# Binary cross-entropy over 8192 x 8192: the last big store moves to GpSimd's queue, and two of the three closing clips move behind other work on VectorE

## The chip, the core and the metric

One core of a Trainium2 chip runs the whole program. The metric is the device time of one execution in microseconds, median of the runs shown; lower is better. The kernel uses VectorE (DVE) and ScalarE (ACT) for arithmetic. Transfers between the device memory and the on-chip memory are issued by GpSimd (POOL), SyncE (SP) and, at the very start, ScalarE, and are carried out by the core's 16 DMA engines.

## What is computed

Two matrices of 8192 x 8192 float32, `pred` in (0.01, 0.99) and `target` of zeros and ones:

```
pred = clip(pred, 1e-7, 1 - 1e-7)
out  = -(target * log(pred) + (1 - target) * log(1 - pred))
```

Because `target` is 0 or 1, the kernel computes it as `-log(|target - 1 + pred|)`: for a target of 1 the argument is `pred`, for a target of 0 it is `|pred - 1|`.

## The kernel before

The matrices are treated as one flat run of elements and cut into 36 chunks, numbered k = 0 to 35. A chunk takes the same number of columns on each of 128 partitions: two chunks of 3072 columns, 31 of 16384 (k = 2 to 32, the big ones, 8 MiB of `pred` each), two of 4608 and one of 1024. The last three (k = 33, 34, 35) are called a, b and c in the code and "the small chunks" here.

Two rings in on-chip memory hold the data: `ring_p` in float32 (it takes `pred`, is worked on in place, and is stored as the result) and `ring_t` in bfloat16 (`target`, converted by its load). Each ring has two slots of 16384 columns and a spare of 1024. The big chunks use the two slots in turn. Chunk 31 lies in slot 0, chunk 32 in slot 1. The small chunks a and b lie side by side in slot 0, where chunk 31 was, and c lies in the spare, which nobody used before.

A chunk goes through five operations, each in place:

- `clip` (L89, VectorE), the two bounds in one instruction
- `log`, three instructions: `target - 1 + pred` (L95, VectorE), absolute value (L98, ScalarE), natural logarithm (L99, ScalarE)
- `back` (L103, VectorE), the change of sign

The big chunks are worked on in eight pieces of 2048 columns: clip and log of each piece in turn, and then back of all eight, and then one store. Chunks a and b are clipped whole and otherwise worked on in halves of 2304 columns; c is worked on whole.

The order on every engine is the order of the program text; nothing reorders it. What is loaded ahead is issued by GpSimd, one queue for all of it: in the loop's step k it issues the `target` and then the `pred` load of chunk k + 1, and then, when VectorE has finished with chunk k, its store (`store`, L80). In the last step (k = 32) it issues instead the three `target` loads of a, b, c (L76), and then their three `pred` loads (L73). The `pred` load of a waits until the store of chunk 31, whose slot it takes, has landed. GpSimd's queue, `q0` in the profile, takes up the issued transfers in the order of issue. The function `store` picks the queue: the last four stores (k = 32 to 35) are SyncE's, `q1` in the profile, and all others are GpSimd's. SyncE also waits in order: a store that it issues stands behind the one before it.

The end of the program (L134 to L148) is the part that the change touches: first the three clips of a, b and c, one after the other, and then the logs and backs of the small chunks, with the stores of a, b and c. The store of c is cut by rows into three issues (L85).

Of the kernel before, what the change touches and what calls it, by code (L numbers as in the profile page):

```python
# [1 line left out]

# [4 lines left out]

EPS = 1e-7

BIG = 16 * 1024  # L10
FIRST = 3072
LAST = 4608
TAIL = 1024
SLOTS = 2
PIECES = 8


def plan(total):
    n = (total - 2 * FIRST - 2 * LAST - TAIL) // BIG
    assert n > 4 and total == 2 * FIRST + n * BIG + 2 * LAST + TAIL  # L20
    spots = [(FIRST, 0, 0), (FIRST, FIRST, FIRST)]
    spots += [(BIG, k % SLOTS * BIG, k % SLOTS * BIG) for k in range(1, n + 1)]
    end = (n + 1) % SLOTS * BIG
    spots += [(LAST, end, end), (LAST, end + LAST, end + LAST)]
    return spots + [(TAIL, SLOTS * BIG, SLOTS * BIG)]


@with_exitstack
def kernel(
    ctx: ExitStack,  # L30
    tc: tile.TileContext,
    pred: bass.AP,
    target: bass.AP,
    out: bass.AP,
):
    nc = tc.nc
    fp32 = mybir.dt.float32
    bf16 = mybir.dt.bfloat16
    Alu = mybir.AluOpType
    Act = mybir.ActivationFunctionType  # L40
    P = nc.NUM_PARTITIONS

    R, C = pred.shape
    spots = plan(R * C // P)
    n = len(spots)
    widths = [s[0] for s in spots]
    cols = [sum(widths[:k]) for k in range(n)]

    def chunk(ap, k):
        flat = ap.rearrange("r c -> (r c)")  # L50
        return flat[cols[k] * P : (cols[k] + widths[k]) * P].rearrange("(p w) -> p w", p=P)

    pool = ctx.enter_context(tc.tile_pool(name="rings", bufs=1))
    ring_p = pool.tile([P, SLOTS * BIG + TAIL], fp32, name="ring_p", tag="ring_p")
    ring_t = pool.tile([P, SLOTS * BIG + TAIL], bf16, name="ring_t", tag="ring_t")
    warm = pool.tile([1, 8], fp32, name="warm", tag="warm")

    def spot(k, part=(0, 1)):
        w, c, _ = spots[k]
        i, m = part  # L60
        return ring_p[:, c + i * w // m : c + (i + 1) * w // m]

    def spot_t(k, part=(0, 1)):
        w, _, c = spots[k]
        i, m = part
        return ring_t[:, c + i * w // m : c + (i + 1) * w // m]

    def load_p(k):
        if k == 0:
            for rows in (slice(0, P, 2), slice(1, P, 2)):  # L70
                nc.scalar.dma_start(out=spot(0)[rows], in_=chunk(pred, 0)[rows])
        else:
            nc.gpsimd.dma_start(out=spot(k), in_=chunk(pred, k))  # L73

    def load_t(k):
        nc.gpsimd.dma_start(out=spot_t(k), in_=chunk(target, k))  # L76

    def store(k):
        queue = nc.sync if k >= n - 4 else nc.gpsimd
        queue.dma_start(out=chunk(out, k), in_=spot(k))  # L80

    def store_rows(k):
        src, dst = spot(k), chunk(out, k)
        for first, last in ((0, 108), (108, 120), (120, 128)):
            nc.sync.dma_start(out=dst[first:last], in_=src[first:last])  # L85

    def clip(k, *part):
        p = spot(k, *part)
        nc.vector.tensor_scalar(  # L89
            out=p, in0=p, scalar1=EPS, scalar2=1 - EPS, op0=Alu.max, op1=Alu.min  # L90
        )

    def log(k, *part):
        p = spot(k, *part)
        nc.vector.scalar_tensor_tensor(  # L95
            out=p, in0=spot_t(k, *part), scalar=1.0, in1=p, op0=Alu.subtract, op1=Alu.add
        )
        nc.scalar.activation(out=p, in_=p, func=Act.Abs)  # L98
        nc.scalar.activation(out=p, in_=p, func=Act.Ln)  # L99

    def back(k, *part):
        p = spot(k, *part)
        nc.vector.tensor_scalar(out=p, in0=p, scalar1=-1.0, scalar2=None, op0=Alu.mult)  # L103

    with tc.manual_schedule():
        nc.vector.memset(warm, 1.0)  # L106
        load_t(0)
        load_p(0)
        load_t(1)
        for k in (1, 2):  # L110
            load_p(k)
        load_t(2)
        nc.scalar.activation(out=warm, in_=warm, func=Act.Ln)  # L113
        for k in (0, 1):
            clip(k)
            log(k)
        for k in (0, 1):
            back(k)
            store(k)
        a, b, c = range(n - 3, n)  # L120
        m = PIECES
        for k in range(2, a):
            coming = (k + 1,) if k + 1 < a else (a, b, c)
            for j in coming:
                load_t(j)
            for j in coming:
                load_p(j)
            for i in range(m):
                clip(k, (i, m))
                log(k, (i, m))  # L130
            for i in range(m):
                back(k, (i, m))
            store(k)
        for j in (a, b, c):  # L134
            clip(j)
        log(a, (0, 2))
        log(a, (1, 2))
        log(b, (0, 2))
        back(a, (0, 2))
        log(b, (1, 2))  # L140
        back(a, (1, 2))
        store(a)
        log(c)
        back(b, (0, 2))
        back(b, (1, 2))
        store(b)
        back(c)
        store_rows(c)  # L148


# [1 line left out]
_INS = ['pred', 'target']  # L152
_OUTS = [((8192, 8192), 'float32')]


# [23 lines left out]
```

## Time and profile before

| what | value |
|---|---|
| time, median of 3 runs | 1886.07 us (1885.7 to 1886.33) |
| the profiled execution's own time | 1886.53 us |
| its span, from the first to the last instruction | 1884.7 us |
| VectorE busy | 1171.3 us (62%) |
| ScalarE busy | 954.8 us (51%) |
| HBM read and written over the span | 536.87 MB and 268.44 MB, 427 GB/s |
| transfers of GpSimd's queue q0, SyncE's q1, ScalarE's q10 | 655.89, 13.63 and 1.57 MB |

How to read it: times inside the execution are counted from the start of the span. An instruction's busy time is the time in which its engine worked on it; a transfer is not an instruction, and shows as the time from its issue to its landing. The share of the 16 DMA engines that is busy is given by stretches; values a little over 1 occur, because a stretch counts packets that overlap. The transferred bytes of a `target` load are counted at bfloat16's size, half of what is read from memory, so the GB/s of a stretch with such loads looks low while the DMA engines are fully busy.

The order of instructions around the end, by the trace: chunk 32's last back ends at 1827.16 us; SyncE issues its store at 1827.19 us. The three small `pred` loads are issued between 1809.87 us and 1812.42 us.

### The profile page before, as it was taken

What the parts mean: (1) busy time and instruction counts of PE and PEld (TensorE: products, weight loads), DVE (VectorE), ACT (ScalarE), POOL (GpSimd) and SP (SyncE); (2) the same over time, 40 slices, a digit from 0 to 9 for tenths busy, and PEclk for the clock granted to TensorE, in tenths of its full rate; (3) what the DMA queues carried; (4) which work ended last, traced back from release to release, by engine and by line L of the source; (5) the groups of instructions that cost most, each with busy time, mean ns of one, the idle gap of its engine ahead of it and who ended that gap; (6) DMA issues with size and microseconds to landing.
All of it is one profiled execution on the core that took longest, in us unless ns stands there. A gap on an engine that the chain in (4) does not pass through costs nothing.

```text
span 1884.7 us, 1546 instructions
## 1 busy us (share of the span) xinstructions
DVE 1171.3 (62%) x764; ACT 954.8 (51%) x512; POOL 56.4 (3%) x107
## 2 busy tenths in 40 slices
DVE  3775556755567655577555775556765567755584
ACT  2664336653456544566444664446654456634463
POOL 0000000000000000000000000000000000000000
DMA  9999999999999999999999999999999999999994
GB/s 333 301 334 401 378 349 341 352 371 399 345 353 337 365 392 370 341 351 341 398 378 352 340 351 376 396 353 345 344 362 394 369 344 346 347 392 385 346 369 205
DMA packets 15595, 671.19 MB, mean 356 GB/s; under 512 B 1760, under 2 KB 1760, under 8 KB 2400
## 3 DMA queue, kind: packets, MB, share of 16 engines
q0 software_dynamic: 14832, 655.89, 97.1%
q1 hardware_dynamic: 592, 13.63, 1.7%
q10 hardware_dynamic: 160, 1.57, 0.2%
q14 instruction: 11, 0.09, 0.0%
HBM read 536.87 MB, written 268.44 MB: 427 GB/s over the span
## 4 chain that ended last, share of the span: by engine, by line
DMA 38%; issue 30%; DVE 30%; ACT 1%; POOL 1%; POOLq 0%; DVEq 0%; PEldq 0%
DMA ring_p<-in_pred_dram 34%; DVE ring_p L95 15%; DVE ring_p L89 7%; DVE ring_p L103 7%; DMA out_dram<-ring_p 4%; ACT ring_p L99 1%; ACT ring_p L98 0%; POOL ring_t L76 0%; POOL out_dram L80 0%; POOL ring_p L73 0%; POOLq L80 0%; DVEq L95 0%; PEldq L174 0%; POOLq L73 0%; POOLq L76 0%
## 5 line engine op out<-in xcount | busy, mean ns | idle before, releaser
L98 ACT ACTIVATE ring_p<-ring_p 128x2048 f32<-128x2048 f32 (+2 forms) x255 | 485.1, 1902 | 910.4 <-DVE ring_p L95 910.4
L89 DVE TENSOR_SCALAR ring_p<-ring_p 128x2048 f32<-128x2048 f32 (+2 forms) x253 | 312.1, 1233 | 667.6 <-DMA ring_p<-in_pred_dram 667.6
L95 DVE SCALAR_TENSOR_TENSOR ring_p<-ring_t,ring_p 128x2048 f32<-128x2048 bf16 (+2 forms) x255 | 586.4, 2300 | 27.3 <-DMA ring_t<-in_target_dram 18.8
L99 ACT ACTIVATE ring_p<-ring_p 128x2048 f32<-128x2048 f32 (+2 forms) x255 | 489.0, 1918 | 8.1
L103 DVE TENSOR_SCALAR ring_p<-ring_p 128x2048 f32<-128x2048 f32 (+2 forms) x255 | 293.8, 1224 | 9.0 <-ACT ring_p L99 9.0
L73 POOL DMA_DIRECT2D ring_p<-in_pred_dram x35 | 19.6, 562 | 1209.4 <-DMA out_dram<-ring_p 1209.4
L80 POOL DMA_DIRECT2D out_dram<-ring_p x32 | 17.2, 537 | 545.6 <-DVE ring_p L103 545.6
L76 POOL DMA_DIRECT2D ring_t<-in_target_dram x36 | 19.8, 551 | 0.8 <-PEq L174 0.8
L113 ACT ACT_TABLE_LOAD x1 | 1.3, 1283 | 2.0 <-issue 2.0
L106 DVE MEMSET warm<- 1x8 f32 x1 | 0.1, 65 | 0.8 <-PEq L163 0.8
L113 ACT ACTIVATE warm<-warm 1x8 f32<-1x8 f32 x1 | 0.2, 208 | 0.0
L163 POOL MEMSET const-float32-0.0<- 128x1 f32 x1 | 0.1, 98 | 0.2 <-issue 0.2
L163 POOL MEMSET const-bfloat16-1.0<- 128x1 bf16 x1 | 0.1, 101 | 0.0
L163 POOL MEMSET const-float32-1.0<- 128x1 f32 x1 | 0.1, 99 | 0.0
L163 POOL MEMSET const-uint8-127<- 128x1 uint8 x1 | 0.1, 98 | 0.0
## 6 DMA issues: line engine op xcount, KB each, us to landing
ring_t<-in_target_dram POOLq DMA_DIRECT2D x31, 4096.0 KB, 58.9
ring_p<-in_pred_dram POOLq DMA_DIRECT2D x2, 2304.0 KB, 23.5
out_dram<-ring_p SPq DMA_DIRECT2D x2, 2304.0 KB, 7.2
out_dram<-ring_p POOLq DMA_DIRECT2D x2, 1536.0 KB, 35.0
ring_t<-in_target_dram POOLq DMA_DIRECT2D x2, 1152.0 KB, 47.5
ring_p<-in_pred_dram ACTq DMA_DIRECT2D x2, 768.0 KB, 6.9
ring_t<-in_target_dram POOLq DMA_DIRECT2D x2, 768.0 KB, 11.5
ring_p<-in_pred_dram POOLq DMA_DIRECT2D x1, 1536.0 KB, 16.1
```

Source lines behind the costliest of these rows:

```text
L73: nc.gpsimd.dma_start(out=spot(k), in_=chunk(pred, k))
L76: nc.gpsimd.dma_start(out=spot_t(k), in_=chunk(target, k))
L80: queue.dma_start(out=chunk(out, k), in_=spot(k))
L89: nc.vector.tensor_scalar(out=p, in0=p, scalar1=EPS, scalar2=1 - EPS, op0=Alu.max, op1=Alu.min)
L95: nc.vector.scalar_tensor_tensor(out=p, in0=spot_t(k, *part), scalar=1.0, in1=p, op0=Alu.subtract, op1=Alu.add)
L98: nc.scalar.activation(out=p, in_=p, func=Act.Abs)
L99: nc.scalar.activation(out=p, in_=p, func=Act.Ln)
L103: nc.vector.tensor_scalar(out=p, in0=p, scalar1=-1.0, scalar2=None, op0=Alu.mult)
L106: nc.vector.memset(warm, 1.0)
L113: nc.scalar.activation(out=warm, in_=warm, func=Act.Ln)
L163: nc = _bacc.Bacc("TRN2", target_bir_lowering=False, num_devices=1)
```

## The change

Two edits.

In `store`, the bound for SyncE's queue moves by one, so that the store of chunk 32 is GpSimd's. In GpSimd's order it comes behind the three `pred` loads of a, b and c, as its last transfer. SyncE is left with the stores of a, b and c.

At the end of the program the three clips no longer stand together. The clip of a stays where it was. The clip of b moves behind both additions (L95) of a, right in front of b's first. The clip of c moves behind the first store, right in front of c's addition. Nothing else moves, and no operation is added or removed.

```diff
     def store(k):
-        queue = nc.sync if k >= n - 4 else nc.gpsimd
+        queue = nc.sync if k >= n - 3 else nc.gpsimd
         queue.dma_start(out=chunk(out, k), in_=spot(k))
...
-        for j in (a, b, c):
-            clip(j)
+        clip(a)
         log(a, (0, 2))
         log(a, (1, 2))
+        clip(b)
         log(b, (0, 2))
         back(a, (0, 2))
         log(b, (1, 2))
         back(a, (1, 2))
         store(a)
+        clip(c)
         log(c)
         back(b, (0, 2))
         back(b, (1, 2))
```

## The prediction

> **What bounds the kernel now.** I read the shares of the page first: VectorE is busy 62% and ScalarE 51% of the span, while the row of DMA slices is 9 (90% or more) in every slice but the last, which is 4. So the kernel is bound by its transfers up to the last slice of 47 us, and both edits lie there. The view of busy time by stretches, over the end (columns: stretch, its length, busy time of VectorE, ScalarE and GpSimd, granted clock, DMA share, GB/s):
>
> ```profile
> 1770.00:1790.00 20.00, 0.00 (x0) 0.00 (x0) 1.62 (x4) 1.00 1.02 442
> ...
> 1840.00:1847.00 7.00, 2.56 (x1) 0.00 (x0) 0.00 (x0) 1.00 1.02 441
> 1847.00:1849.00 2.00, 0.00 (x0) 0.00 (x0) 0.00 (x0) 1.00 0.24 100
> 1849.00:1851.00 2.00, 0.00 (x0) 0.00 (x0) 0.00 (x0) 1.00 0.08 35
> 1851.00:1853.30 2.30, 0.02 (x1) 0.00 (x0) 0.00 (x0) 1.00 0.02 7
> 1853.30:1866.40 13.10, 13.10 (x8) 9.87 (x5) 0.00 (x0) 1.00 0.00 0
> ...
> 1881.00:1882.50 1.50, 0.00 (x0) 0.00 (x0) 0.00 (x0) 1.00 0.70 227
> 1882.50:1883.50 1.00, 0.00 (x0) 0.00 (x0) 0.00 (x0) 1.00 0.49 184
> 1883.50:1884.70 1.20, 0.00 (x0) 0.00 (x0) 0.00 (x0) 1.00 0.00 0
> ```
>
> The engines that move data are full until 1847, then all but one or two are done (0.08 of 16 engines is 1.3), and one trails until about 1853. From 1853.3 to 1866.4 nothing at all is moved, while VectorE is busy throughout. Why VectorE is busy only then stands in the timeline:
>
> ```profile
> 1827.34 2.56 DVE L89 TENSOR_SCALAR ring_p<-ring_p 128x4608 f32<-128x4608 f32 x1 [0.18 <-DMA ring_p<-in_pred_dram]
> 1840.01 2.56 DVE L89 TENSOR_SCALAR ring_p<-ring_p 128x4608 f32<-128x4608 f32 x1 [10.11 <-DMA ring_p<-in_pred_dram]
> 1853.28 0.69 DVE L89 TENSOR_SCALAR ring_p<-ring_p 128x1024 f32<-128x1024 f32 x1 [10.71 <-DMA ring_p<-in_pred_dram]
> 1853.88 7.49 DVE L95 SCALAR_TENSOR_TENSOR ring_p<-ring_t,ring_p 128x2304 f32<-128x2304 bf16 x3
> 1856.47 2.12 ACT L98 ACTIVATE ring_p<-ring_p 128x2304 f32<-128x2304 f32 x1 [32.55 <-DVE ring_p L95]
> ```
>
> Chunk a is clipped at 1827.34, but its addition stands behind the clips of b and c, which wait 10.11 and 10.71 us for their loads. ScalarE idles 32.55 us with it. The loads of b and c are late because the big store runs beside them from 1827.19. That is in the list of transfers (size, median us from issue to landing):
>
> ```profile
> ring_p<-in_pred_dram POOLq DMA_DIRECT2D x2, 2304.0 KB, 23.5
> out_dram<-ring_p SPq DMA_DIRECT2D x2, 2304.0 KB, 7.2
> ring_p<-in_pred_dram POOLq DMA_DIRECT2D x1, 512.0 KB, 42.4
> ...
> out_dram<-ring_p SPq DMA_DIRECT2D x1, 25.6
> ```
>
> The last row is the big store (8192 KB): 1827.19 + 25.6 = 1852.8. The 512 KB load of c was issued at 1810.90 and landed 42.4 later, at 1853.25, with the store.
>
> **The change, part by part.** First the rate. The store of chunk 31 ran alone on the DMA engines after the load of 32 (landed 1790.28, where VectorE's next clip begins) until 1809.58 (the chain of waits): 8192 KB in 19.3 us, 424 KB/us. Between 1827.3 (a landed) and 1853.2 the loads of b and c and the big store moved 2304 + 512 + 8192 = 11008 KB in 25.9 us, 425 KB/us. These are times of the trailing engine, which ends each of them; 424 is its pace, times 16.
>
> *The store's queue.* One issue of 0.54 us (GpSimd's mean for L80) leaves SyncE and joins GpSimd. In GpSimd's queue it passes no one: the three loads are issued by 1812.42, before chunk 32 is ready at 1827.2, and behind it stands only the end of the program. In front of SyncE's store of a stands nothing now. The bytes are the same, but they are taken up in another order: b's load needs 2304 / 424 = 5.4 us after a, so it lands at 1832.7 instead of 1840.0; c's 1.2 more, 1833.9 instead of 1853.25; and then the big store, 19.3, until 1853.2, as before. Cover for a late start of it: the trailing engine has loads until 1833.9, 6.7 us after the issue; other engines end their loads some 5 us earlier (the trail in the stretches from 1847 to 1853) and would idle first, which costs nothing as long as the trailing one is not caught up.
>
> *The clips.* VectorE from 1827.34, durations of the same shapes (clip 2.56, addition 7.49 / 3 = 2.50, back 1.35; for c 0.69, 1.22, 0.69): clip a to 1829.9; additions of a to 1832.4 and 1834.9; clip b (landed 1832.7, no wait) to 1837.5; b's first addition 1840.0; back of a's first half 1841.3 (ScalarE is done with it at 1832.4 + 2 x 2.12 = 1836.7); b's second addition 1843.8; back of a's second half 1845.2, and a's store is issued, 21.2 us earlier than its 1866.4 now. Clip c to 1845.9 and its addition to 1847.1, with up to 0.5 for the gap that stood between clip c and the next addition (1853.45 to 1853.88 in the chain). ScalarE goes from 1840.9 through b's halves, done at 1845.2 and 1849.4, and c, done at 1851.5. Back of b's second half then ends at 1850.8 and b's store is issued (now 1874.7); back of c at 1852.2 (now 1876.0). Removed: the two waits, 20.8 us on the path. Added: no instruction and no wait; clip b and c cost the same 2.56 and 0.69 as before, now beside transfers instead of behind them.
>
> *What sets the end then.* Not that chain: the transfers. A store takes about 7.2 - 5.4 = 1.8 us more than its bytes, so a's data flow from about 1847, inside the big store; b's from 1852.6, before the trailing engine can be through with the big store and a (1853.2 + 5.4 = 1858.6); c's likewise. So the trailing engine never idles, and it is done at 1853.2 + 4608 / 424 (10.9) + c's part. An even share of c is 512 / 424 = 1.2; a cut into 108, 12 and 8 rows need not be even over 16 engines, so the bound below is 0. I take the middle, 0.6: 1864.7. From the last transfer to the end of the span it was about 1.1 (busy to 1883.5 or a little more, end at 1884.7). Span 1865.8, 18.9 less than 1884.7. With the 1.83 that lie around the span (1886.53 - 1884.7) the profiled execution would take 1867.6; the median of the runs lies 0.46 below the profiled one, so **1867.2**.
>
> The Trainium skill, "DMA: Bandwidth & Descriptors", section "Latency and other measured facts", states that DMA engines 7 and 15 are usually slower than the rest; and its section "Why a DMA increments its semaphore by 16 and not by 1", that a transfer issued by SyncE runs on the lowest-numbered engines, as many as divide its partitions, 12 for 108. The trailing engine of the rows above fits the first; if it is 15, c's part on it is 0 and the time 1866.6; if it is 7, 512 / 12 KB at a sixteenth of 424 are 1.6, and the time is 1868.2.
>
> Bounds of what the trace does not show, a store of GpSimd's beside one of SyncE's: full pace on one side; on the other the 409 GB/s of the stretch 1829 to 1840, where loads of the one queue met the store of the other, against 441 after it, over the 18 us from 1847: 1.4 more. If a last piece of 64 KB of the big store (65536 bytes, one row of 16384 columns) stood by itself at the end, 64 / 26.5 = 2.4 more. Below: c's part 0 and the tail 0.7, 1 less, and some spread.
>
> **Rivals.**
>
> *The queue's order does not matter* (the change does not do the first thing it says): the loads land as before, 1840.0 and 1853.25. For it: a queue's transfers overlap where pieces are small. Against: the loads of a and b came one after the other. VectorE then clips b to 1842.6 and issues a's store at 1850.3; clip c, its addition and b's backs end near 1858.4, b's data flow from 1859.8, 1.2 after the trailing engine is free: 1868.4. The clips alone bring nearly all.
>
> *The store's start is held up by VectorE.* GpSimd issues it at 1827.2, exactly when VectorE takes up clip a, and VectorE then works without a break to 1852. The three load issues at 1809.87, beside a busy VectorE, took 2.55 us against 1.61 for the three at 1770.02 beside an idle one; whether their data also came later is hidden by the backlog. If it were held until VectorE's last back, the trailing engine would idle from 1833.9 until a's store at 1846.6, 12.7 us, and the time be 1867.2 + 12.7 + 1 = 1880.9. Against it: each big load of the loop is issued amid VectorE's work (at 1751.91 between pieces), and the DMA share stays at 0.94 or more. The Trainium skill, "SBUF — State Buffer", section "SBUF: two separate sides", names this: while VectorE runs in a mode that uses the port it shares with GpSimd, GpSimd cannot write descriptors. By that rule a single clip holds it for 2.56 us, which the 6.7 us of cover take.
>
> *Two queues of stores disturb each other, slower than before.* Place: from 1846.6 on, where a's store meets the rest of the big one. Left to move then: 6.6 us of the big store and 5120 KB, 18.7 us at full pace. The old traffic ended at 1883.5, 36.9 us later; so it decides at half the pace, some 215 KB/us. At 0.45 of it the time is 1890. For it: no row shows two queues of stores at once. Against: the loads of one beside the store of the other ran at 409 and 441 GB/s.
>
> **How the numbers follow.** Forecast 0.86, loads as before 0.06 (1868.4), start held up 0.04 (up to 1880.9), stores disturbing each other 0.04 (near 1886 or above). The likeliest gives 1867.2. Up to 1871.5 for the 1.4 and 2.4 of the bounds, down to 1864.5; that takes in the first rival and leaves out less than 2 in 10. A measurement of this kernel tells 0.2%, 3.8 us, from no change. Faster by more: the first three cases, 0.96; of the last, 0.01 within 0.2% and 0.03 slower.
>
> **What would show it.** Right: clip a followed at once by two additions; clip b with no wait and c's load landed by about 1834; a's store issued near 1845 and c's near 1852; no stretch between 1827 and 1864 with a DMA share near 0; the last instruction near 1866. Wrong: clip c waiting for its load (the order of the queue), a hole in the DMA share between 1834 and 1846 (start held up), GB/s well under 400 from 1847 to 1859 with all engines busy (stores disturbing each other), or VectorE or ScalarE still at work after 1860.

## The result, and the profile after

The changed kernel takes 1869.12 us (median of 4 runs, 1868.35 to 1869.34), the kernel before beside it 1886.2 us (1885.7 to 1887.71). The ratio is 0.9907, with a 95% interval of 0.989 to 0.9925: 17.1 us less. The forecast was 1867.2 us in a range of 1864.5 to 1871.5. The profiled execution of the changed kernel took 1868.35 us, its span 1866.6 us.

The timeline of its end (start, length, engine, line, tile, shape, idle time before):

```profile
1826.27 2.56 DVE L89 TENSOR_SCALAR ring_p<-ring_p 128x4608 f32<-128x4608 f32 x1 [0.18 <-DMA ring_p<-in_pred_dram]
1826.38 2.57 POOL L80 DMA_DIRECT2D out_dram<-ring_p  x1 [15.05 <-DVE ring_p L103]
1828.86 5.03 DVE L95 SCALAR_TENSOR_TENSOR ring_p<-ring_t,ring_p 128x2304 f32<-128x2304 bf16 x2
...
1833.81 2.55 DVE L89 TENSOR_SCALAR ring_p<-ring_p 128x4608 f32<-128x4608 f32 x1
...
1843.88 0.69 DVE L89 TENSOR_SCALAR ring_p<-ring_p 128x1024 f32<-128x1024 f32 x1
...
1843.99 6.11 SPq L80 DMA_DIRECT2D out_dram<-ring_p  x2
...
1851.03 4.19 SPq L85 DMA_DIRECT2D out_dram<-ring_p  x3
```

Of the three clips only a's has an idle time in front of it, 0.18 us; the 10.11 and 10.71 us of before are gone. The first small store is issued at 1843.99 instead of 1866.4, c's at 1851.03 instead of 1876.05. The second line is GpSimd's issue of the big store; it took 2.57 us, as long as the clip beside it, where such issues took 0.54 us on average before.

The transfers (size, median us from issue to landing):

```profile
ring_p<-in_pred_dram POOLq DMA_DIRECT2D x2, 2304.0 KB, 19.9
out_dram<-ring_p SPq DMA_DIRECT2D x2, 2304.0 KB, 14.0
ring_p<-in_pred_dram POOLq DMA_DIRECT2D x1, 512.0 KB, 23.1
...
out_dram<-ring_p POOLq DMA_DIRECT2D x1, 27.2
```

The load of c, issued at 1809.8 behind those of a and b, landed 23.1 us later, at 1832.9 (1853.25 before). The big store landed at 1826.38 + 27.2 = 1853.6. Everything at the end of this execution lies some 1.1 us earlier than in the kernel before (a's clip at 1826.27 for 1827.34), so by the distance from a's clip it landed later: 27.3 us for 1852.8 - 1827.34 = 25.5. A small store now takes 14.0 us to land for 7.2: it is issued early and waits its turn.

The busy time by stretches (stretch, length, VectorE, ScalarE, GpSimd, granted clock, DMA share, GB/s). A stretch counts a DMA packet wholly where the packet begins, and a row of the big store is one packet of 2.4 us, so a share can be over 1, and too low in the stretch behind:

```profile
1829.00:1846.60 17.60, 17.53 (x10) 15.02 (x8) 0.00 (x0) 1.00 1.07 462
1846.60:1859.00 12.40, 2.55 (x3) 3.64 (x3) 0.00 (x0) 1.00 0.89 379
1859.00:1861.00 2.00, 0.00 (x0) 0.00 (x0) 0.00 (x0) 1.00 0.85 285
1861.00:1863.00 2.00, 0.00 (x0) 0.00 (x0) 0.00 (x0) 1.00 0.55 193
1863.00:1865.00 2.00, 0.00 (x0) 0.00 (x0) 0.00 (x0) 1.00 0.06 23
1865.00:1866.60 1.60, 0.00 (x0) 0.00 (x0) 0.00 (x0) 1.00 0.01 3
```

VectorE works through the first stretch beside the transfers. The 13 us with no transfer at all are gone, and the arithmetic is over at 1851, 15 us ahead of the end. What is left at the end is a DMA share of 0.06 from 1863 to 1865, about one engine of 16. The landings in the trace agree: 15 engines are through with the store of c by 1863.7, and the last one lands at 1865.7.

### The profile page after: what moved, and what is told of

The parts are those of the page before. It is cut to its first block, busy times and chain, and to the rows that moved or that the text cites. A ratio compares the mean times of both kernels' runs of the same rounds, so it can differ in the third digit from the quotient of the medians.

```text
span 1866.6 us, 1546 instructions
## 1 busy us (share of the span) xinstructions
DVE 1171.4 (63%) x764; ACT 954.8 (51%) x512; POOL 59.0 (3%) x108
## 4 chain that ended last, share of the span: by engine, by line
DMA 37%; issue 30%; DVE 30%; ACT 1%; POOL 1%; POOLq 0%; DVEq 0%; PEldq 0%
DMA ring_p<-in_pred_dram 33%; DVE ring_p L95 15%; DVE ring_p L89 8%; DVE ring_p L103 7%; DMA out_dram<-ring_p 4%; ACT ring_p L99 1%; ACT ring_p L98 0%; POOL ring_t L76 0%; POOL out_dram L80 0%; POOLq L80 0%; DVEq L89 0%; PEldq L175 0%; POOLq L73 0%; POOLq L76 0%
## 5 line engine op out<-in xcount | busy, mean ns | idle before, releaser
L95 DVE SCALAR_TENSOR_TENSOR ring_p<-ring_t,ring_p 128x2048 f32<-128x2048 bf16 (+2 forms) x255 | 586.6, 2301 | 27.3 <-DMA ring_t<-in_target_dram 18.7
```

The costliest lines, as they stand in the source:

```text
L95: nc.vector.scalar_tensor_tensor(out=p, in0=spot_t(k, *part), scalar=1.0, in1=p, op0=Alu.subtract, op1=Alu.add)
```

## The experiments

The theory: the end is set by the DMA engine that trails, and all that the change has to do is bring the small stores in time, so that this engine never idles. A measure that does not depend on when a's load landed in an execution (1826 to 1829): from the start of a's clip to the first closing drain of SyncE (DRAIN in the profile, an instruction that every engine has at the end of the program), which stands 0 to 0.3 us behind the last landing in these traces. In the kernel before it is 1883.9 - 1827.34 = 56.6 us, in the changed one 1865.8 - 1826.27 = 39.5.

**One edit alone, and more work on VectorE.** These four ran side by side, with the kernel before at 1886.68 us. The changed kernel again:

> The changed kernel again, as the base of the runs beside it: 1869.1 us as measured (1868.35 to 1869.34). Both theories say the same of it.

Measured: 1869.79 us (1868.19 to 1871.16), ratio 0.991 (0.9895 to 0.9925). Single executions of this kernel lie up to 3 us apart, more than those of the kernel before (1.1 us in this set, 2.0 in the first).

The queue alone:

```diff
-        queue = nc.sync if k >= n - 4 else nc.gpsimd
+        queue = nc.sync if k >= n - 3 else nc.gpsimd
...
         for j in (a, b, c):
             clip(j)
```

> The big store on GpSimd's queue, the three clips together as before. Theory of the transfers (the end is set by the trailing DMA engine, which is never idle once stores arrive in time): c's load lands near 1833, so the clips no longer wait, a's store is issued near 1848, b's near 1855.6 and c's near 1857, all before the trailing engine is free for them; time within 1 us of the changed kernel, 1869 to 1870. Rival (each edit brings its own share of the 20.8 us of waits that are gone, so one alone brings about half): 1877 to 1879.

Measured: 1868.59 us, ratio 0.9904 (0.9889 to 0.9918): 18.1 us less than before, where the whole change brings 16.9 in this set; it is a little under the 1869 to 1870 expected. The timeline shows that the clips no longer wait for the big store:

```profile
1827.44 2.56 DVE L89 TENSOR_SCALAR ring_p<-ring_p 128x4608 f32<-128x4608 f32 x1 [0.17 <-DMA ring_p<-in_pred_dram]
...
1832.84 3.16 DVE L89 TENSOR_SCALAR ring_p<-ring_p 128x4608 f32<-128x4608 f32 x2 [2.84 <-DMA ring_p<-in_pred_dram]
...
1848.44 8.62 SPq L80 DMA_DIRECT2D out_dram<-ring_p  x2
...
1858.08 2.89 SPq L85 DMA_DIRECT2D out_dram<-ring_p  x3
```

The clips of b and c (one row, x2) begin 5.4 us after a's; a's store is issued at 1848.44 and c's at 1858.08. Counted from a's clip that is 21.0 and 30.6 us, against 17.7 and 24.8 in the changed kernel: 3 and 6 us later, at no cost.

The clips alone, with the big store still SyncE's:

```diff
-        for j in (a, b, c):
-            clip(j)
+        clip(a)
         log(a, (0, 2))
         log(a, (1, 2))
+        clip(b)
...
         store(a)
+        clip(c)
```

> The clips moved, the big store on SyncE's queue as before. Theory of the transfers: b's load lands near 1840 and c's near 1853 as before, a's store is issued near 1850, b's near 1858.4, its data 1.2 us after the trailing engine is free; 1 to 2 us over the changed kernel, 1870 to 1871. Rival (each edit its own share): 1877 to 1879.

Measured: 1870.06 us, ratio 0.9911 (0.9895 to 0.9928), 16.6 us less than before. Its timeline:

```profile
1840.82 2.56 DVE L89 TENSOR_SCALAR ring_p<-ring_p 128x4608 f32<-128x4608 f32 x1 [5.03 <-DMA ring_p<-in_pred_dram]
...
1854.10 0.69 DVE L89 TENSOR_SCALAR ring_p<-ring_p 128x1024 f32<-128x1024 f32 x1 [3.12 <-DMA ring_p<-in_pred_dram]
...
1859.22 2.79 SPq L85 DMA_DIRECT2D out_dram<-ring_p  x3
```

The loads of b and c still come late, at 1840.8 and 1854.1, and their clips still wait, 5.03 and 3.12 us; yet the gain is only 0.3 us short of that of both edits, and 1.5 short of that of the queue alone (expected were 1 to 2 us short of both). Both edits remove the same hole by different means, and the two gains do not add: 18.1 and 16.6 alone, 16.9 together in the same set. The rival, a share for each edit, falls.

Two more clips of a, which lengthen the chain on VectorE by 5.1 us:

```diff
-        clip(a)
+        for _ in range(3):
+            clip(a)
```

> The changed kernel with two more clips of a behind its first (they change no value), 2 x 2.56 = 5.1 us more work on VectorE ahead of everything that follows. Theory of the transfers: a's store is issued near 1849, b's near 1855, c's near 1856, all still ahead of the trailing engine, so no more than 0.5 us over the changed kernel. Rival (the chain through VectorE and ScalarE sets the end): 5.1 us more, 1874. A side question: the issue of the big store on GpSimd took 2.57 us beside one clip; if VectorE gives way between two instructions it takes about 2.6 again, if it holds GpSimd off through all three it takes 7.7, and the trailing engine runs out of loads 1 us before.

Measured: 1869.52 us, ratio 0.9908 (0.9894 to 0.9923): no cost beside 1869.79.

In a second set (kernel before: 1886.99 us) the same with four more, `range(5)`:

> The changed kernel with four more clips of a (no value changes), 10.2 us more work on VectorE. Theory of the transfers: a's store is issued near 1854.2 and its data flow from 1855.6, some 3.4 us after the trailing engine is through with the big store; 3 to 5 us over the changed kernel, 1872 to 1874. Rival (the chain sets the end): 10.2 more, 1879.

Measured: 1873.53 us (1873.1 to 1874.0), ratio 0.993 (0.9915 to 0.9945), 3.7 to 4.4 over the changed kernel, as the theory said. The timeline and the stretches of the profile:

```profile
1828.30 12.94 DVE L89 TENSOR_SCALAR ring_p<-ring_p 128x4608 f32<-128x4608 f32 x5 [0.18 <-DMA ring_p<-in_pred_dram]
1828.41 2.57 POOL L80 DMA_DIRECT2D out_dram<-ring_p  x1 [15.05 <-DVE ring_p L103]
...
1856.40 6.03 SPq L80 DMA_DIRECT2D out_dram<-ring_p  x2
```

```profile
1829.00:1851.00 22.00, 21.79 (x9) 7.07 (x4) 1.98 (x1) 1.00 0.90 389
1851.00:1857.80 6.80, 6.77 (x6) 6.77 (x4) 0.00 (x0) 1.00 0.12 53
```

Here a's store comes at 1856.40, after the big one is through, and the hole is back: a DMA share of 0.12 for 6.8 us. So the chain has some 6 us of slack in the changed kernel; it costs nothing inside it, and beyond it the excess. The side question is answered by the second line: beside five clips in a row the issue took 2.57 us, as beside one and beside three. GpSimd is held through one clip, not through all.

That it is the length of the clip that counts shows at another place of the changed kernel, where the three small `pred` loads are issued beside VectorE's work:

```profile
1807.78 2.29 DVE L95 SCALAR_TENSOR_TENSOR ring_p<-ring_t,ring_p 128x2048 f32<-128x2048 bf16 x1
1808.80 2.54 POOL L73 DMA_DIRECT2D ring_p<-in_pred_dram  x3 [38.24 <-DMA out_dram<-ring_p]
...
1809.99 1.22 DVE L89 TENSOR_SCALAR ring_p<-ring_p 128x2048 f32<-128x2048 f32 x1
```

```profile
L73 POOL DMA_DIRECT2D ring_p<-in_pred_dram x35: 527/532/1502, 2.4 to 1809.8; - x35
```

The first two of the three lie inside an addition of 2.29 us and took 0.53 and 0.55 us, as most issues do (median 0.53). The third, from 1809.83, is the longest of all (1.50 us): a clip of 1.22 us began beside it, and it ended 0.1 us after that clip, as the issue of the big store ended 0.1 us after its clip of 2.56.

**What lies in the last microseconds.** The store of c by one issue:

```diff
-        for first, last in ((0, 108), (108, 120), (120, 128)):
+        for first, last in ((0, 128),):
```

> The changed kernel with c stored by one issue of 128 rows. If the trailing engine, which in the changed kernel carried a part of every one of c's three issues (up to 11 rows of 4 KB), sets the end, it now carries 8: 3 x 4 KB at its pace, 0.5 us less, 1868.6. Rival (the cut of c has nothing to do with the end): same as the changed kernel.

Measured: 1868.28 us, ratio 0.9902 (0.9887 to 0.9917). And by 119, 7 and 2 rows, `((0, 119), (119, 126), (126, 128))`:

> The changed kernel with c cut into 119, 7 and 2 rows. If an issue of SyncE runs on as many engines as divide its rows, the lowest ones, 119 and 7 rows run on the first seven, 18 rows each. If the trailing engine is not among these, the end is b's landing, 1.8 us less: 1867.3. If it is among them, it carries 18 rows for 11, 1.1 us more: 1870.2. If the cut has nothing to do with the end: same as the changed kernel.

Measured: 1869.98 us, ratio 0.9911 (0.9896 to 0.9926). Both go the way of a trailing engine that carries rows of c, but in the times by no more than the executions differ. By the measure from a's clip on, the one issue takes 1864.9 - 1826.79 = 38.1 us, the 119 rows 1867.0 - 1827.16 = 39.8, and the changed kernel 39.5 and (second profile) 39.4.

The single DMA packets of the trace, which the views only add up, show the rows themselves. A row of c is one packet of 4 KB, 0.16 us, and the engine that finishes last has its rows in unbroken succession behind its last packet of b: eleven rows in 1.73 us in the changed kernel (1863.57 to 1865.30, and the same in two more profiles of it), eight rows in 1.25 us with one issue, and eighteen in 2.80 us with 119, 7 and 2. So the trailing engine does carry rows of c, and in the numbers that the two expectations had worked out. Each issue's landings come from 12, 12 and 8 engines in the changed kernel, and from 7, 7 and 2 with 119 rows.

All stores on GpSimd's queue:

```diff
     def store(k):
-        queue = nc.sync if k >= n - 3 else nc.gpsimd
-        queue.dma_start(out=chunk(out, k), in_=spot(k))
+        nc.gpsimd.dma_start(out=chunk(out, k), in_=spot(k))
...
-            nc.sync.dma_start(out=dst[first:last], in_=src[first:last])
+            nc.gpsimd.dma_start(out=dst[first:last], in_=src[first:last])
```

> The changed kernel with the stores of a, b and c on GpSimd's queue too. Theory of the transfers: order and bytes on the trailing engine stay, each issue may be held up to 2.6 us by VectorE, and none is on the path but c's, so 1868 to 1871. Rival (two queues of stores disturb each other, and that is the 1.9 us by which the changed kernel took longer than forecast): 1867.

Measured: 1873.64 us (1871.4 to 1874.27), ratio 0.9926 (0.991 to 0.9943). Both theories missed: it is about 4 us slower than the changed kernel. The closing instructions of its profile tell why (durations in ns, least, median and longest; first and last start in us):

```profile
L174 POOLq DRAIN  x3: 46/90/17583, 1854.2 to 1872.2; - x3
L174 SPq DRAIN  x3: 7/7/7, 1867.6 to 1872.0; - x3
```

SyncE saw the last landing just before 1867.6, 39.3 us after a's clip (the landing itself is at 1867.3): the data were no later. But GpSimd's closing drain lasted from 1854.2 for 17.58 us, to 1871.8, and the span ended at 1872.5. In the changed kernel the same two lines are

```profile
L175 POOLq DRAIN  x3: 46/93/31525, 1826.4 to 1866.3; - x3
L175 SPq DRAIN  x3: 7/7/7, 1865.8 to 1866.1; - x3
```

There the long drain ended at 1826.4 + 31.5 = 1857.9, which is 4.3 us after the big store landed (1853.6), and 8 us ahead of SyncE's.

**Settling what was open.** A third set in five rounds, kernel before at 1886.77 us:

> The changed kernel in five rounds, beside the three below on one chip: 1869 to 1870, from 1869.12 and 1869.79 measured.

Measured: 1869.81 us (1867.72 to 1870.47), ratio 0.9909 (0.9895 to 0.9923); 38.8 us from a's clip to the last landing.

> The store's queue alone, clips together, again. Theory of the transfers (the second edit brings nothing once the loads of b and c come first): within 0.8 us of the changed kernel on either side. Rival (the clips bring a part of their own that the three rounds could not show): over 1 us slower than the changed kernel.

Measured: 1868.46 us (1867.24 to 1869.07), ratio 0.9903 (0.9889 to 0.9917). The second edit brings nothing on top of the first; the median is even 1.35 us lower without it, as it was 1.2 us lower in the first set, a little outside the 0.8 of the theory. The intervals overlap. From a's clip to the last landing both profiles with the queue alone have 38.7 us, beside 38.8 to 39.5 in the changed kernel; why the median should be lower was not found.

> The changed kernel with c stored by one issue of 128 rows, again. Theory (the trailing engine's rows of c are part of the end): its last landing is 38.0 to 38.4 us after a's load, against 39.4 and 39.5 in two profiles of the changed kernel, and the time 0.5 to 1.5 us under that of the changed kernel. Rival (chance between executions): the same as the changed kernel.

Measured: 1868.65 us (1867.57 to 1868.97), ratio 0.9904 (0.989 to 0.9918), 1.2 under the changed kernel beside it, with intervals that overlap, and 1866.4 - 1828.23 = 38.2 us from a's clip, against 38.1 in the first profile of it.

The diff of the last one, stores of a and b on GpSimd's queue too and c's on SyncE's:

```diff
-        queue = nc.sync if k >= n - 3 else nc.gpsimd
+        queue = nc.sync if k >= n - 1 else nc.gpsimd
```

> The changed kernel with the stores of a and b on GpSimd's queue too, c's on SyncE's. In the run with all stores on one queue the last data landed at 1867.3, as in the changed kernel, but GpSimd's closing drain went on 4.5 us longer. Theory of the drain (it ends 4.2 to 4.5 us after the last landing of GpSimd's own queue, and holds up the end where that is late): b lands near 1865.6, the drain ends near 1870, the span near 1870.6, 1871.5 to 1872.5 in time. Rival (GpSimd's queue moves the small stores more slowly): the data land over 2 us later than in the changed kernel, and the drain costs nothing of its own. Second rival (only c on GpSimd's queue matters): same as the changed kernel.

Measured: 1873.27 us (1872.46 to 1874.03), ratio 0.9928 (0.9914 to 0.9942), somewhat over the 1871.5 to 1872.5 of the drain theory. Its closing instructions:

```profile
L175 POOLq DRAIN  x3: 46/102/19465, 1852.0 to 1872.0; - x3
L175 SPq DRAIN  x3: 7/7/7, 1867.2 to 1871.8; - x3
```

The last landing, that of b's store, lies just before 1867.2, 38.8 us after a's clip and so no later than in the changed kernel; c's, in SyncE's queue, lies 0.2 us ahead of it. GpSimd's drain ends at 1852.0 + 19.5 = 1871.5, 4.4 us after b's landing, and the span at 1872.3. So in two kernels the span ends behind this drain and not behind the data: it is not the place of c's store, and not slower data. What GpSimd does in these 4.4 us the trace does not show.

## Why the prediction was right, and where its sum was short

**The bound.** Right. The transfers set the end once the hole of 13 us is filled; two more clips at no cost, and four at 4 us, show the slack of the chain and where it ends.

**The order of the queue.** Right. The loads of a, b and c came one behind the other, and c's landed 6.7 us after a's, as worked out; the rival in which the order does not matter falls. That the clips alone would bring nearly all, which that rival said in passing, is what the run with the clips alone showed, 1.7 us off its figure. What the prediction did not ask is the reverse: the queue alone brings as much as both edits, so one of the two edits was enough.

**The chain on VectorE and ScalarE.** Right within 0.2 us: against a's clip, which began 1.07 us earlier in this execution, a's store was forecast for 1844.1 and came at 1843.99, c's for 1851.1 and came at 1851.03.

**The start of the big store.** The rival's mechanism is real, its size is not. The issue lasted as long as the clip beside it, to 1828.95, and the trailing engine had loads to move until c's landed at 1832.9, so the hold cost nothing. The Trainium skill, "SBUF — State Buffer", section "SBUF: two separate sides", has GpSimd wait for one such instruction of VectorE, and the trace agrees: 2.57 us beside one clip, beside three and beside five. In the run with the queue alone, where that engine's packets can be followed one by one, its first row of the big store begins 0.01 us after its last packet of c's load, and it stands still nowhere from there to the end. That the store landed 27.3 us after a's clip, for 25.9 in the working, has another reason: a's store landed only 4.1 us behind it, where its bytes take 5.4, so part of a's data went ahead of the end of the big store.

**Two queues of stores.** No disturbance seen. With one queue the last landing came 39.3 us after a's clip, with two 38.8 to 39.5.

**The end.** This is the term that was mis-sized. The working gave 1864.7 - 1827.34 = 37.4 us from a's clip to the last landing; three profiles have 39.5, 39.4 and 38.8. I had taken half of an even share of c for the trailing engine, 0.6 us, out of a range from 0 to the even share of 1.2. It carries more than an even share: eleven of the 128 rows, where an even share is eight, and they took 1.73 us. That is 1.1 of the missing 1.4 to 2.1. In the first two profiles most of the rest is one packet: the trailing engine's last packet of b took 1.48 and 1.39 us (0.74 in the third), where its packets of that size take 0.69. It took 1.37 us with all stores in one queue as well, so the second queue is not the reason; what is, is not known. Stored in one issue of even parts, c gives 38.1 and 38.2, which is the working with the full share of 1.2 (38.0); so the cut into three issues costs 0.6 to 1.4, of which 0.5 is the three rows more. The tail behind it was 0.9 us for the 1.1 assumed. With 39.2 for 37.4 the forecast becomes 1868.8; measured were 1869.1 to 1869.8. The sum came within 2 us although the measured share of c lies outside the two bounds that it took for it.

The estimate with an uneven cut drawn from the Trainium skill, 1868.2 with the trailing engine in c's share at 1.6 us, came nearer than the middle, and its 1.6 is close to the 1.73 measured. Which engine that is, is another question. By the Trainium skill, "DMA: Bandwidth & Descriptors", section "Why a DMA increments its semaphore by 16 and not by 1", an issue of 119 rows runs on the seven lowest engines; the trace agrees on the number, seven landings, and does not name the engines. If they are the lowest, the eighteen rows that the trailing engine carried in that run put it among those seven there, and it was neither 7 nor 15. In the changed kernel it carried a row of the issue of 8 rows as well, which would put it among the eight lowest.

What the prediction did not see at all is GpSimd's closing drain. A store moved to that queue has to land more than 4 us ahead of the rest, or the drain behind it holds up the end. The move of the big store was safe by some luck: the drain ended 8 us ahead of the end, as the stores of a, b and c came after it.

## What to carry to other kernels

Two edits against one idle stretch of the bounding resource did not add here: find the stretch first, and ask of each edit whether it fills it alone. In the last stage order transfers by what waits for them: a large store that nobody waits for belongs behind the small loads that everybody waits for, and an in-order engine should not stand at a late load while earlier data lie ready. When the transfers bind, take the pace and the share of the slowest DMA engine down to the last kilobyte, and keep GpSimd's queue out of the last microseconds of a program.

## What the runs showed of the hardware that was not expected

- GpSimd's closing drain ended 4.3 to 4.5 us after the last landing of that engine's own queue, in the changed kernel (1857.9 after 1853.6) and where it was late enough to matter (1871.8 after 1867.3; 1871.5 after 1867.1). There the kernels took 3.5 to 4.5 us longer than the changed one.
- An issue of GpSimd's beside a clip of 2.56 us on VectorE took 2.57 us for 0.54, and one beside a clip of 1.22 us took 1.50; both ended 0.1 us after the clip. With five clips in a row it took no longer: GpSimd gets in between two instructions. Beside an addition of 2.29 us an issue took 0.53 us, as most issues do.
- One DMA engine trails the others, by about 2 us at the end of the changed kernel and 5 us around 1850 in the kernel before, and it alone sets the end of the changed kernel. The cut of the last store decides its part there: 8, 11 or 18 rows of 4 KB, 1.25, 1.73 or 2.80 us.
